# The last phase of a streaming encoder layer: o and z loaded apart, y in halves from a bound, gates read a step ahead

## The chip, the cores and the metric

The kernel runs on one core of a Trainium2 chip. The metric is device time in microseconds (us) of one execution; the number for a kernel is the median of several. Beside it one execution was taken by the hardware profiler: its span is the time from the first to the last instruction of the program, its own time includes what lies around that.

A core has five engines with an instruction queue each, worked off in order: TensorE (PE, with PEld for its weight loads), VectorE (DVE), ScalarE (ACT), GpSimd (POOL) and SyncE (SP). In this kernel nearly all DMAs are issued by SP, so an issue that waits holds up every DMA issue behind it.

## The reference, cut to what matters

One layer, for 2,048 prompt frames and 8 sample streams of 16 frames, `D_MODEL` = 1024. The attention outputs `oa`, `ob` and the projections `za`, `zb`, `ga`, `gb` are there; the last phase computes:

```python
def merge_branches(oa, ob, za, zb, ga, gb, subln_g, lam_init, w_branch_a, w_branch_b, w_out):
    oa = rms_norm(oa, subln_g) * (1.0 - lam_init)
    ya = (oa.reshape(b, s, WIDTH_A) * jax.nn.silu(za)) @ w_branch_a
    yb = (ob.reshape(b, s, WIDTH_B) * jax.nn.silu(zb)) @ w_branch_b
    return (jax.nn.sigmoid(ga) * ya + jax.nn.sigmoid(gb) * yb) @ w_out
...
        xp = xp + gate * merge_branches(...)
...
    y_prompt = rms_norm(xp, final_g)
```

`WIDTH_A` = `WIDTH_B` = 512. The same is done for the sample frames.

## The kernel before, in words

All tensors are float32. A matmul operand is split into two float16 parts, hi and lo, after a scaling by a power of two (`scales` makes it from a sum of squares, with tiny DVE instructions; `split` writes hi on ACT or POOL and lo on DVE, L284 to L292). A product is then three chains of matmuls: hi x hi, hi x lo, lo x hi.

The program has two large parts. The first projects tiles of 128 frames and runs both attentions for eight units; it writes each tile's attention output to `o_d`, z to `z_d` and the gates' pre-activations to `g_d` in HBM. The second, the last phase (from L1305 on, `with ExitStack() as c2`), takes 17 tiles (`tiles`: 15 prompt tiles, the sample tile NT = 16, then the last prompt tile) through a pipeline, one step n for each:

- `inputs(t)` (L1160): loads o, z and g; u = o * z * sigmoid(z), normed for the first half by `orms`. POOL multiplies o by z in two halves (L1175), ACT takes sigmoid of z into a PSUM bank of kind "mm" (L120 is the helper `act`), DVE multiplies (L1177, L1181). ACT takes the sigmoid of the gates in place. Then the sum of squares (L274), the scale, and the split of u into `u16` (L287, L292), which lies in `hs[2]`; o and z lie in `hs[0]` and `hs[1]`.
- `turned(st)` (L1193): a DMA transpose of `u16` into `st["u"]`, one of two buffers.
- `branches(st)` (L1198): four pieces (half j of the columns, branch br) of 12 matmuls (L1207); DVE scales by `iu` and multiplies by the gate (L1209), POOL adds the two branches (L1211). After the last, `finish` squares both halves on ACT, makes the scale `sy`, and splits y into `y16`.
- `turned_y(st)` (L1230): one DMA transpose of `y16` into the one buffer `L["y"]`.
- `output(t, st)` (L1331): loads the x rows (L1337), two halves of 24 matmuls with w_out (L1344), DVE scales by `iy` and the adaLN gate (L1348), POOL adds x (L1352), then ACT squares, DVE makes the root and scales (L1357), and the rows are stored (L1358).

Tiles overlap: step n multiplies the branches of tile n, the output of tile n - 1, and prepares tile n + 2. The pieces of a step have costs, and `interleave` merges them by these with those of a second stream, `lane`: the attention of the sample streams (`sample`, L701), spread over steps 0 to 12 (`S_TILES` = 13). It loads cache tiles of 512 KB, transposes keys on TensorE (L735, copied out at L736), makes scores (L745, L752), weights (L770, L776), and values (L788), with sigmoid, scan (L607) and products of its own on ACT, DVE and POOL. The program order made so is what a scheduler with a simulated timeline starts from; from there each engine has a fixed order.

PSUM has eight banks, by kind: "mm" 2, "s" 3, "t" 1, "o" 2. The sample stream's queries (L721) and weights `wn` (L776) take "t", of which there is one.

`early_work` puts the inputs of the first two tiles and the branches of the first among the last attention steps. Step order of the pieces before:

```python
            if 0 < n <= NT:
                work += branches(states[tiles[n]])
            if n + 1 <= NT:
                work.insert(2, (0.9, lambda n=n: turned(states[tiles[n + 1]])))
            if n + 2 <= NT:
                work.insert(5, (0.1, lambda n=n: states.update({tiles[n + 2]: inputs(tiles[n + 2])})))
            if n > 0:
                work += output(tiles[n - 1], states.pop(tiles[n - 1]))
            if 0 < n <= NT:
                work.append((0.9, lambda n=n: turned_y(states[tiles[n]])))
```

## Time and profile before

| | |
|---|---|
| median of 3 runs | 2289.36 us (2288.38 to 2291.46) |
| profiled execution, its own time | 2288.94 us |
| its span | 2287.2 us, mean granted TensorE clock 0.966 |
| first and last matmul of the branches (L1207) | 1752.6 and 2249.8 us |
| first and last matmul of the output (L1344) | 1792.7 and 2276.3 us |

Busy time is given by engine; PE's includes the depth of its pipeline. A row of waits names the engine and line that stood idle, then what ended the wait. In rows of the trace a square bracket gives the idle time before an instruction and what released it; "issue" means that nothing the profile shows was waited for. Tile names are those of the buffers: `wa`, `wb` are the 4 KB buffers in which the last phase keeps gates, y16, u and y transposed and the branch weights; `hs` holds o, z and u16; `dk`, `dks`, `dsc` belong to the sample stream. The granted clock is TensorE's, as a share of full speed.

### The profile page before, as it was taken

The page shows a single profiled execution, that of the slowest core. Times are in us where ns is not written, and L with a number is a line of the kernel's source. Part 1 is how long each engine was busy: PE and PEld are TensorE (multiplying, and loading weights), DVE is VectorE, ACT ScalarE, POOL GpSimd, SP SyncE. Part 2 cuts the span into 40 slices and gives each one's busy share as a digit, 9 for nine tenths or more (in the row PEclk, how much of TensorE's full clock was granted, in tenths as well). Part 3 has the DMA queues.
Part 4 walks back from the last instruction along what each step waited for, and adds up shares of the span by engine and source line. Part 5 has one row for each costly group of instructions (what it writes and reads, how often), then busy time and mean ns, then how long its engine had stood idle before and what let it go on. Part 6 is the DMA issues. An engine that isn't in the chain of part 4 may idle for free.

```text
span 2287.2 us, 40620 instructions
## 1 busy us (share of the span) xinstructions
PE 2083.3 (91%) x14478; PEld 1111.4 (49%) x14478; DVE 1606.7 (70%) x3523; ACT 1483.5 (65%) x2968; POOL 689.8 (30%) x575
## 2 busy tenths in 40 slices
PE   4998999998999999899989989999986789988997
PEld 2554554554555455455545545555543344444443
DVE  4668666788886678978667797876777655555654
ACT  3877677788767677877667777666776444444431
POOL 1522013255301235530023463012344222232331
PEclk7998999999999999999999999999996899999998
DMA  8667668697775778875576887657687989887662
GB/s 295 212 214 184 151 144 219 155 211 171 190 161 121 168 144 205 178 187 124 124 174 147 193 179 176 150 138 167 145 184 171 295 220 253 213 222 199 186 157 74
DMA packets 764267, 411.93 MB, mean 180 GB/s; under 512 B 525498, under 2 KB 709098, under 8 KB 763552
## 3 DMA queue, kind: packets, MB, share of 16 engines
q1 hardware_dynamic: 762986, 408.86, 72.9%
q8 instruction: 113, 1.85, 0.3%
q14 instruction: 90, 0.74, 0.1%
q10 hardware_dynamic: 1078, 0.48, 0.1%
HBM read 211.53 MB, written 72.91 MB: 124 GB/s over the span
## 4 chain that ended last, share of the span: by engine, by line
PE 57%; DVE 13%; DMA 9%; ACT 8%; issue 8%; POOL 3%; SPq 1%; POOLq 0%; DVEq 0%; ACTq 0%
PE ps_mm L423 20%; PE ps_mm L495 12%; PE ps_mm L1207 5%; PE ps_o L1344 5%; PE ps_s L630 3%; PE ps_s L631 3%; DVE sc_n L607 3%; DMA wt<-sc_n 2%; ACT junk L274 2%; ACT sc_p L120 1%; PE ps_o L682 1%; DMA wb<-wa 1%; POOL sc_p L613 1%; DMA hs<-o_d 1%; DVE wb L292 1%
## 5 line engine op out<-in xcount | busy, mean ns | idle before, releaser
L423 PE MATMUL ps_mm<-wb,hs 128*128 128x512 f16 x2244 | 559.6, 382 | 7.3 <-DVE v L292 3.9
L613 POOL TENSOR_TENSOR sc_p<-sc_p,sc_n 128x127 f32<-128x127 f32 (+7 forms) x192 | 306.9, 1603 | 779.7 <-DVE sc_n L607 769.9
L423 PEld LDWEIGHTS <-hs 128*128 128x128 f16 x2928 | 256.7, 98 | 237.1 <-issue 14.8
L495 PE MATMUL ps_mm<-wa,hs 128*128 128x512 f16 x1224 | 307.4, 379 | 0.0
L607 DVE TENSOR_TENSOR_SCAN sc_n<-ps_s,sc_n,zero_t 128x512 f32<-128x512 f32 x192 | 245.5, 1279 | 68.2 <-ACT ps_s L120 66.1
L120 ACT ACTIVATE sc_p<-ps_s,usc 128x512 f32<-128x512 f32 (+3 forms) x320 | 202.6, 633 | 98.3 <-PE ps_s L631 60.6
L630 PE MATMUL ps_s<-k,qst 128*128 128x512 f16 (+3 forms) x640 | 226.4, 354 | 40.3 <-DVE sc_n L607 36.9
L562 DVE TENSOR_TENSOR sc_n<-sc_p,sc_n 128x128 f16<-128x128 f32 (+7 forms) x192 | 212.0, 1110 | 41.2 <-ACT sc_n L561 40.8
L631 PE MATMUL ps_s<-k,qst 128*128 128x512 f16 (+3 forms) x640 | 226.6, 355 | 0.0
L1344 PE MATMUL ps_o<-wo,wb 128*128 128x512 f16 x816 | 195.8, 395 | 24.5 <-DMA wb<-wa 21.1
L682 PE MATMUL ps_o<-v,wt 128*128 128x128 f16 x1088 | 192.1, 224 | 25.1 <-DMA wt<-sc_n 25.0
L495 PEld LDWEIGHTS <-hs 128*128 128x128 f16 x1632 | 140.2, 98 | 119.7 <-issue 0.5
L120 ACT ACTIVATE ps_s<-ps_s,usc 128x512 f32<-128x512 f32 (+3 forms) x320 | 194.2, 607 | 0.0
L561 ACT CAST sc_n<-sc_p 128x128 f16<-128x128 f32 (+7 forms) x192 | 153.6, 805 | 57.6 <-POOL sc_p L613 57.4
L683 PE MATMUL ps_o<-v,wt 128*128 128x64 f16 x1088 | 173.3, 197 | 0.0
L423 PE MATMUL ps_mm<-wa,hs 128*128 128x512 f16 x684 | 168.9, 379 | 0.0
L682 PEld LDWEIGHTS <-wt 128*128 128x128 f16 x1088 | 106.7, 101 | 106.7 <-DMA wt<-sc_n 33.9
L1344 PEld LDWEIGHTS <-wb 128*128 128x128 f16 x816 | 81.1, 101 | 127.8 <-DMA wb<-wa 24.3
L683 PEld LDWEIGHTS <-wt 128*128 128x128 f16 x1088 | 104.7, 100 | 72.2 <-issue 1.4
L457 POOL TENSOR_TENSOR rot<-pr,rope 128x256 f32<-128x256 f32 x68 | 63.3, 931 | 251.4 <-ACT pr L437 204.3
L607 DVE TENSOR_TENSOR_SCAN sc_n<-ps_s,zero_t 128x128 f32<-128x128 f32 (+3 forms) x128 | 104.6, 818 | 47.4 <-ACT ps_s L120 46.1
L274 ACT ACTIVATE junk<-wa 128x1024 f16<-128x1024 f32 (+1 forms) x73 | 66.7, 914 | 103.9 <-POOL wa L1211 66.5
(328 smaller groups left out, 4273.7 us busy)
## 6 DMA issues: line engine op xcount, KB each, us to landing
hs<-hT_d SPq DMA_DIRECT2D x122, 512.0 KB, 4.2
g_d<-gt SPq DMA_DIRECT2D x68, 256.0 KB, 3.8
wa<-in_w_in_dram SPq DMA_DIRECT2D x52, 256.0 KB, 5.0
out_dram<-pr SPq DMA_DIRECT2D x204, 64.0 KB, 1.8
wa<-g_d SPq DMA_DIRECT2D x25, 512.0 KB, 5.4
wide<-in_w_ada_dram SPq DMA_DIRECT2D x12, 1024.0 KB, 8.4
z_d<-pr SPq DMA_DIRECT2D x136, 64.0 KB, 2.0
o_d<-o SPq DMA_DIRECT2D x136, 64.0 KB, 2.6
```

The lines of the kernel that those rows point to most:

```text
L120: i = S.activation(**kw)
L423: T.matmul(box["p"], box["h"][:, hi, k, :], U["w"][k][:, wi, :], start=(n == 0), stop=(n == 3 * KT - 1))
L495: T.matmul(box["g"][:, 0:gw], box["h"][:, hi, k, :], U["wg"][k // per][:, k % per, wi, :], start=(j == 0), stop=(j == 3 * KT - 1))
L561: S.copy(out=hi, in_=src)
L562: V.tensor_tensor(out=lo, in0=src, in1=hi, op=ALU.subtract)
L607: V.tensor_tensor_scan(out=dst[:, lo : lo + n][:, ::-1], data0=src[:, 0:n][:, ::-1], data1=zero_t[:, 0:1].to_broadcast([P, n]), initial=fi ...
L613: G.tensor_tensor(out=p[:, 0:m], in0=p[:, 0:m], in1=n[:, 1 : m + 1], op=ALU.mult)
L630: T.matmul(p[:, 0:n], qst[:, c, :], kk[:, c, 0:n], start=True, stop=False)
L631: T.matmul(p[:, 0:n], qst[:, 2 + c, :], kk[:, c, 0:n], start=False, stop=not diag)
L682: T.matmul(po[:, c * P : (c + 1) * P], wt[:, wj, :], vt[:, c, :, :], start=first, stop=False)
L683: T.matmul(po[:, c * P : c * P + 64], wt[:, nb + wj, :], vt[:, c, 0, :], start=False, stop=last)
L1344: T.matmul(po, st["y"][:, yi * 8 + k, :], wo[j * 4 + k // 2][:, wi, k % 2, :], start=(n == 0), stop=(n == 3 * KT - 1))
```

## The change

- o is loaded at the start of a step (`started`), z after the second branch piece; `inputs` then works on both. POOL multiplies o by z in one instruction, placed in its order after POOL's last sum of the branches (`L["sum"]`, an order without a wait); DVE's multiplications come after the last split of y (`L["low"]`).
- sigmoid of z is written over z, no more into a PSUM bank, and `u16` then takes z's buffer `hs[1]`.
- y's scale comes from a bound, the sum of squares of u times that of the branch weights (`wf`), so `sy` and `iy` are made in `inputs`; each half of y is split as soon as it is summed, into the gate buffer that it has freed, and has a transpose of its own. The transposed y has two buffers. The output's matmuls go through the k of half 0 first.
- the rows of a tile are normed (`normed`) and stored (`stored`) a step later; x is loaded a step before it is used, into three buffers in turn (`hs[2]` is the third).
- gates are loaded at the end of step n for tile n + 2 (`gated`), and their sigmoid is taken in step n + 1 (`opened`).
- the transposition of u moves from the middle of the step after to the end of the same step.
- in the sample stream, the transposes of queries and of `wn` take a bank "s" instead of "t".

```diff
@@ queries, weights
-            pt = bank("t")
+            pt = bank("s")
@@
+    def started(t):
+        m = len(begun) % 2
+        begun.append(t)
+        load(out=hs[0], in_=o_d[t])
+        return dict(t=t, u=L["u"][m], home=L["g"][2 * m : 2 * m + 2], yT=L["y"][m])
+
-    def inputs(t):
+    def inputs(st):
         o, z = hs[0:2]
-        load(out=o, in_=o_d[t])
-        load(out=z, in_=z_d[t])
...
-        for n in range(2):
-            c = slice(n * 512, (n + 1) * 512)
-            sg = bank("mm")
-            act(out=sg, in_=z[:, c], func=AF.Sigmoid)
-            G.tensor_tensor(out=o[:, c], in0=o[:, c], in1=z[:, c], op=ALU.mult)
-            if n == 1:
-                V.tensor_tensor(out=o[:, c], in0=o[:, c], in1=sg, op=ALU.mult)
...
-        for g in gs:
-            act(out=g, in_=g, func=AF.Sigmoid)
+        i = G.tensor_tensor(out=o, in0=o, in1=z, op=ALU.mult)
+        if "sum" in L:
+            tc.add_manual_dep(i.ins, L["sum"].ins.name, NOSYNC, reason="order of tiles")
+        act(out=z, in_=z, func=AF.Sigmoid)
+        for h in range(4):
+            c = slice(h * P, (h + 1) * P)
+            i = V.scalar_tensor_tensor(out=o[:, c], in0=z[:, c], scalar=r[:, h : h + 1], in1=o[:, c], op0=ALU.mult, op1=ALU.mult)
+            if "low" in L:
+                tc.add_manual_dep(i.ins, L["low"].ins.name, NOSYNC, reason="order of tiles")
+        V.tensor_tensor(out=o[:, 512:D], in0=o[:, 512:D], in1=z[:, 512:D], op=ALU.mult)
...
+        V.tensor_tensor(out=yb, in0=acc, in1=L["wf"], op=ALU.mult)
+        sy = scales(yb, tiny, "sy")
...
-        u16 = hs[2].bitcast(F16).rearrange("p (f n) -> p f n", f=2)
+        u16 = z.bitcast(F16).rearrange("p (f n) -> p f n", f=2)
...
+    def gated(st):
+        st["g"] = [b.rearrange("p (b n) -> p b n", b=2) for b in st["home"]]
+        for j in range(2):
+            load(out=st["g"][j], in_=g_d[st["t"]].rearrange("p (b n) -> p b n", b=2)[:, :, j * 512 : (j + 1) * 512])
+
+    def opened(st):
+        for g in st["g"]:
+            act(out=g, in_=g, func=AF.Sigmoid)
@@ branches
-                G.tensor_tensor(out=g, in0=st["g"][j][:, 0, :], in1=g, op=ALU.add)
-                if j == 1:
-                    finish()
-        def finish():
...
+                L["sum"] = G.tensor_tensor(out=g, in0=st["g"][j][:, 0, :], in1=g, op=ALU.add)
+                y16 = st["home"][j].bitcast(F16)[:, 0:D]
+                L["low"] = split(y16[:, 0:512], y16[:, 512:D], g, st["sy"][:, 0:1], S)
@@
-    def turned_y(st):
-        st["y"] = yT = L["y"].bitcast(F16).rearrange("p (k n) -> p k n", n=P)
-        nc.sync.dma_start_transpose(out=yT, in_=st["y16"].rearrange("p f n -> p (f n)"))
+    def turned_y(st, j):
+        st["y"] = yT = st["yT"].bitcast(F16).rearrange("p (k n) -> p k n", n=P)
+        nc.sync.dma_start_transpose(out=yT[:, j * KT : (j + 1) * KT, :], in_=st["home"][j].bitcast(F16)[:, 0:D])
@@ early_work
-            states[t] = inputs(t)
-            if t == tiles[0]:
-                turned(states[t])
+            states[t] = started(t)
+            load(out=hs[1], in_=z_d[t])
+            inputs(states[t])
+            turned(states[t])
+            gated(states[t])
+            opened(states[t])
@@ output
-                for yi, wi in ((0, 0), (0, 1), (1, 0)):
-                    for k in range(KT):
-                        T.matmul(po, st["y"][:, yi * 8 + k, :], wo[j * 4 + k // 2][:, wi, k % 2, :], start=(n == 0), stop=(n == 3 * KT - 1))
+                for half, yi, wi in [(half, yi, wi) for half in range(2) for yi, wi in ((0, 0), (0, 1), (1, 0))]:
+                    for k in range(half * 4, half * 4 + 4):
+                        T.matmul(po, st["y"][:, half * KT + yi * 4 + k % 4, :], wo[j * 4 + k // 2][:, wi, k % 2, :], start=(n == 0), stop=(n == 3 * KT - 1))
...
-                    load(out=y_rows(t), in_=x)
+                    late.append((x, t))
@@ the steps
+            work = [(0.1, lambda: states.update({new: started(new)}))] if more else []
+            work += fro[:2] + [(0.1, normed)]
+            if more:
+                work.append((0.1, lambda: load(out=hs[1], in_=z_d[new])))
+            work += fro[2:] + to[:1] + [(0.1, stored)]
+            if 0 < n < NT:
+                work.append((0.1, lambda: opened(states[tiles[n + 1]])))
+            if n <= NT:
+                work.append((0.1, lambda: with_x(n)))
+            if more:
+                work.append((0.1, lambda: inputs(states[new])))
+            if fro:
+                work.append((0.5, lambda: turned_y(states[tiles[n]], 0)))
+            work += to[1:]
+            if fro:
+                work.append((0.5, lambda: turned_y(states[tiles[n]], 1)))
+            if more:
+                work.append((0.9, lambda: turned(states[new])))
+                work.append((0.1, lambda: gated(states[new])))
             interleave(work, aside(n))
+        normed()
+        stored()
```

`fro` are the four branch pieces of tile n, `to` the two output halves of tile n - 1, and `new` is tile n + 2.

More of the change, by code (lines that the diff above doesn't have):

```diff
@@ L774, in weights @@
                     in_=pt.rearrange("p (j i r s) -> p j i r s", j=4, r=2, s=NS)[:, :, :, r, :])
-            pt = bank("t")
+            pt = bank("s")
             T.transpose(pt[:, 0:P], w[:, 512:640], ident)
@@ L1241, in branch_weight @@
         if i == 0:
-            L["s"] = [scales(total(add_up(wsums[:, lo : lo + 8], 8)), con, f"s_w{lo}") for lo in (0, 8)]
+            sums = [total(add_up(wsums[:, lo : lo + 8], 8)) for lo in (0, 8)]
+            L["wf"] = con.tile([P, 1], F32, name="wf")
+            V.tensor_copy(out=L["wf"], in_=sums[0])
+            L["s"] = [scales(x, con, f"s_w{lo}") for x, lo in zip(sums, (0, 8))]
             L["sa"] = con.tile([P, 1], F32, name="sa")
@@ L1329, in gate_rows, with with_x, normed, stored @@
             return pg
+        def with_x(n):
+            t = tiles[n]
+            states[t]["x"] = x = hs[2] if n % 3 == 2 else s2.tile([P, D], F32, tag="x", name="x2", bufs=2)
+            load(out=x, in_=x_rows(t))
+        late, ready = [], []
+        def normed():
+            while late:
+                x, t = late.pop(0)
+                acc = tiny.tile([P, 1], F32, tag="facc", name="facc")
+                sum_squares(x, D, acc)
+                r = rsqrt_one(acc, D, tiny, "rF")
+                V.scalar_tensor_tensor(out=x, in0=x, scalar=r, in1=fg, op0=ALU.mult, op1=ALU.mult)
+                ready.append((x, t))
+        def stored():
+            while ready:
+                x, t = ready.pop(0)
+                load(out=y_rows(t), in_=x)
         def output(t, st):
-            box = {}
             def half(j):
-                if j == 0:
-                    box["x"] = s2.tile([P, D], F32, tag="x", name="x2", bufs=2)
-                    load(out=box["x"], in_=x_rows(t))
-                x = box["x"]
+                x = st["x"]
                 c = slice(j * 512, (j + 1) * 512)
```

53 lines of the change are left out of this document (13 added, 40 removed).

## The prediction

> **What bounds the kernel now.** I read the page first, then the busy time by stage, then the two lines of matmuls of the last phase, then who waited for whom in it, and last the instructions in order of time around the longest waits.
>
> ```profile
> span 2287.2 us, 40620 instructions
> PE 2083.3 (91%) x14478; PEld 1111.4 (49%) x14478; DVE 1606.7 (70%) x3523; ACT 1483.5 (65%) x2968; POOL 689.8 (30%) x575
> ```
>
> The diff touches only what runs after 1752.6 us (first matmul of L1207) and a little just before it, so I split that part: first two tiles, the tiles that share their steps with the sample stream, the tiles without it, and the end.
>
> ```profile
> core 0: us, PE busy (x) PEld busy (x) DVE busy (x) ACT busy (x) POOL busy (x), PEclk, DMA share, GB/s
> 1752.60:1800.00 47.40, 37.78 (x189) 17.41 (x190) 26.79 (x56) 18.88 (x30) 14.88 (x14) 0.86 0.99 263
> 1800.00:2166.40 366.40, 322.83 (x2469) 170.12 (x2468) 209.31 (x569) 162.99 (x311) 107.13 (x78) 0.95 0.85 222
> 2166.40:2250.10 83.70, 80.52 (x376) 36.22 (x373) 47.33 (x124) 28.53 (x48) 23.21 (x18) 1.00 0.56 147
> 2250.10:2287.20 37.10, 23.31 (x90) 9.17 (x87) 12.96 (x36) 5.62 (x10) 6.28 (x5) 0.83 0.18 56
> ```
>
> TensorE is the fullest engine in every stage, but between 1800 and 2166.4 it idles 366.4 - 322.8 = 43.6 us and its granted clock is 0.95. DVE, ACT and POOL are far from full; the DMA share of 0.85 is high. The same stage for L1207 alone and then for L1344 alone (busy time and count are PE's), and one row of L1344:
>
> ```profile
> 1800.00:2166.40 366.40, 125.08 (x528) 52.03 (x528) 0.95 0.85 222
> 1800.00:2166.40 366.40, 127.21 (x529) 52.14 (x528) 0.95 0.85 222
> L1344 PE MATMUL ps_o<-wo,wb x816: 379/379/634, 1792.7 to 2276.3; 128*128 128x512 f16 x164
> 2229.27 8.15 PE L1344 MATMUL ps_o<-wo,wb 128*128 128x512 f16 x37
> ```
>
> A tile has 48 matmuls of each line, so 528/48 = 11 tiles take 366.4 us, 33.3 us each. At full speed 37 matmuls take 8.15 us, so one start to the next is (8.15 - 0.379)/36 = 0.216 us. The stage's 1,057 matmuls need 228 us, the other PE work 322.8 - 125.1 - 127.2 = 70.5 us: a floor of 299 us, 27.2 us a tile. The stage after it, without the sample stream, has almost no slack (80.5 of 83.7 busy). So the gain to be had lies in the 67 us between 366 and 299, plus the two ends. What PE waits for from 1752 us on:
>
> ```profile
> PE ps_o L1344 <- DMA wb<-wa: 21.1, 8, 4.8
> PE ps_s L735 <- DVE dsc L607: 10.7, 3, 5.5
> PE ps_t L776 <- DVE dks L736: 10.2, 2, 5.1
> ```
>
> and what the queues behind these waits stand for (engine and line, what was waited for: us, times, longest):
>
> ```profile
> ACT wa L120 <- DMA wa<-g_d: 46.8, 20, 6.4
> ACT wb L120 <- DMA wb<-g_d: 26.0, 7, 9.3
> POOL hs L1175 <- DMA hs<-o_d: 57.5, 8, 13.2
> SPq L1358 <- DVE x L1357: 73.6, 12, 18.4
> SPq L1337 <- DMA out_dram<-x: 38.4, 13, 5.8
> ```
>
> **The change, part by part.**
>
> *Price of an idle gap.* After a gap of 5.1 us:
>
> ```profile
> 2007.03 0.48 PE L776 MATMUL ps_t<-ident,dsc 128*128 128x128 f32 x1 [5.12 <-DVE dks L736]
> 2007.29 7.27 PE L1344 MATMUL ps_o<-wo,wb 128*128 128x512 f16 x23
> 2004.80:2011.60 6.80, 4.58 (x12) 1.76 (x13) 4.71 (x17) 3.85 (x9) 2.04 (x2) 0.50 0.51 154
> ```
>
> The granted clock is 0.50 for 6.8 us, and 23 matmuls take 7.27 us where 22 x 0.216 + 0.379 = 5.13 would do: 2.1 us more. At the end of the kernel it is 7.66 - 5.13 = 2.5. I take 2.3 us for each gap of 3 us or more.
>
> *y in halves from a bound.* Before, both halves of g must be squared and summed before either is split, and one transpose carries the whole tile. At the end it reads:
>
> ```profile
> 1900.98 1.46 PE L1344 MATMUL ps_o<-wo,wb 128*128 128x512 f16 x3 [4.03 <-DMA wb<-wa]
> 2250.19 0.75 DVE L1209 SCALAR_TENSOR_TENSOR wa<-ps_mm,iu,wa 128x512 f32<-128x512 f32 x1 [1.84 <-PE ps_mm L1207]
> 2258.17 1.82 SPq L1232 DMA_TRANSPOSE wb<-wa  x1
> 2262.47 7.66 PE L1344 MATMUL ps_o<-wo,wb 128*128 128x512 f16 x23 [3.29 <-DMA wb<-wa]
> ```
>
> From the last scaling (2250.2) to the landing (2262.5) are 12.3 us, covered by only 37 matmuls of the tile before. The change drops the squares on ACT and their sum, splits half 0 while half 1 is still multiplied, and gives yT a second buffer. The chain shrinks to scaling 0.75, POOL's sum 1.25 (half of the 2.49 for two such below), ACT's split 0.7 and DVE's 0.75 (estimates, from the 1,024-wide ones below), landing 4.3 (2258.2 to 2262.5): 7.8 us for the last half, which 8 us of matmuls cover. It could remove all 21.1 us of the eight waits, and three of them are long enough to halve the clock (4.8, 4.03, 3.29): 3 x 2.3 = 6.9, together 28.0. The least is the end and the row at 1901 alone, 3.3 + 4.0 + 4.6 = 12. I take 24: the first wait also stands behind the loads of w_out. The cost is 17 more transposes on SP's queue: 1.82 us at the least for a whole one bounds a half's issue to 0 to 1.8, at most 31 us of SP time, beside a queue that now stands 73.6 + 38.4 us for rows to be normalised and stored. "A step later" and the third x buffer take those two away. I cost the issues at nothing; without that cover each would delay the load behind it by up to 1.8 us.
>
> *Gates one step ahead.* Now ACT stands in order for a gate:
>
> ```profile
> 1852.80 1.06 ACT L120 ACTIVATE wb<-wb 128x1024 f32<-128x1024 f32 x1 [9.35 <-DMA wb<-g_d]
> 1855.76 0.42 DVE L607 TENSOR_TENSOR_SCAN dsc<-ps_s,zero_t 128x128 f32<-128x128 f32 x1 [10.59 <-ACT ps_s L120]
> 1858.10 1.97 PE L735 MATMUL ps_s<-ident,dk 128*128 128x128 f32 x8 [5.51 <-DVE dsc L607]
> 2049.19 1.11 PE L735 MATMUL ps_s<-ident,dk 128*128 128x128 f32 x4 [3.06 <-DVE dsc L607]
> ```
>
> The sample stream's sigmoids stand behind it on ACT, the scan behind those on DVE, and the scan holds the three "s" banks that TensorE needs. That is the 10.7 us of three gaps, two of them over 3 us: 10.7 + 4.6 = 15.3. With the load issued a step earlier ACT does not wait. Bounds 0 (ACT waits for POOL's sum instead) and 15.3; I take 13.
>
> *o and z apart, sigmoid of z in place, order of tiles, two transposes moved from bank "t" to "s".* The gap at 2007 has this chain:
>
> ```profile
> 1996.62 2.49 POOL L1175 TENSOR_TENSOR hs<-hs,hs 128x512 f32<-128x512 f32 x2 [12.31 <-issue]
> 2003.10 1.13 DVE L1181 SCALAR_TENSOR_TENSOR hs<-ps_mm,orms,hs 128x128 f32<-128x128 f32 x4 [8.30 <-ACT ps_mm L120]
> 2006.29 0.68 DVE L736 COPY dks<-ps_t 128x512 f32<-128x512 f32 x1
> ```
>
> POOL stands with the product of the next tile, its sum for the present tile behind it; ACT and DVE follow, and the copy that frees bank "t" comes last. Now the product is put behind the sum, and DVE's four scalings behind the split. The two such gaps cost 10.2 + 4.6 = 14.8. But the moved transposes now share three banks with scan and scores, so the gain is between -5 (one more such gap) and 14.8; I take 7.
>
> *Work itself.* One product of 1,024 instead of two of 512 on POOL, one sigmoid instead of two, four more tiny DVE instructions: nothing on the path, hidden under 27 us of matmuls a tile.
>
> *What is late next.* z's buffer now becomes u16, so the next z can be loaded only when u's transpose has landed. These rows (landing of z; ACT square and split; DVE scalings and split; landing of u's transpose) price the ring:
>
> ```profile
> hs<-z_d SPq DMA_DIRECT2D x12, 512.0 KB, 7.0
> L274 ACT ACTIVATE junk<-hs 128x1024 f16<-128x1024 f32 x16 | 16.9, 1057 | 5.9 <-DVE hs L1177 5.3
> L287 ACT ACTIVATE hs<-hs,su 128x1024 f16<-128x1024 f32 x16 | 18.2, 1137 | 1.3 <-DVE su L225 1.3
> L1181 DVE SCALAR_TENSOR_TENSOR hs<-ps_mm,orms,hs x56: 337/343/352, 1767.2 to 2208.5; 128x128 f32<-128x128 f32 x56
> L292 DVE SCALAR_TENSOR_TENSOR hs<-hs,su,hs x16: 1277/1284/2306, 1757.6 to 2217.5; 128x1024 f16<-128x1024 f32 x16
> DMA to landing us min/median/max: 4.4/6.5/7.5
> ```
>
> 7.0 + 2.5 (product) + 4 x 0.34 + 0.69 (an estimate: half a 1,024 operation of 1.28, rounded up) + 1.06 + about 1 (five tiny instructions) + 1.14 + 1.28 + 6.5 = 22.5 us. My step would be (366.4 - about 35)/11 = 30 us, so the ring has 7 us to spare and I cost it at 0, with up to 3 us a tile (33 us) if each of its seven hops stands in a queue for 1.5 us.
>
> L1181 reads PSUM now and is steady (337 to 352 ns); L292 reads two SBUF tensors and reaches 2,306 against 1,277. The scalings become such operations, so they may take 1.8 times as long, at most 1.6 us a tile more, inside the ring's slack. The Trainium skill's page "SBUF — State Buffer", section "Who interferes with whom", gives the reason: a DVE operation with two SBUF inputs contends with a POOL operation that reads SBUF, and the one issued second is blocked for the whole of the other. The spread of L292 agrees; by that rule alone the sum would lose at most 11 x 1.6 = 18 us, and only if the ring binds.
>
> *Before 1752 us.* Two tiles are now fully opened and turned in the last attention steps, with a transpose and gate loads on SP among the attention's own. No row shows it; the nearest are PE's 9.6 us of idle in the first stage (47.4 - 37.8). Bounds -6 (a better start) and +12 (two landings of 6.5 us, with SP standing); I take +3.
>
> *Sum:* 24 + 13 + 7 - 3 = 41 us. The profiled execution took 2288.94 us, 0.4 below the median of the runs, so about 2248.
>
> **The rivals.**
>
> *Half a gain.* TensorE's y waits go, but ACT, DVE and POOL only change the instruction they stand for, since all three stay in order and the sample stream's banks do not grow. For it: of ACT's 72.8 us on gates TensorE felt only 10.7. Then about 19 of y (between 12 and 28) less the 3 before 1752 us: -16, 2273.
>
> *TensorE at its floor.* All gaps close: 28.0 + 15.3 + 14.8 and 7 us of small ones, -65, 2224. Against it: with some 60 of that in the sampled stage its DMA share would become 0.85 x 366/306 = 1.02.
>
> *The ring binds, slower.* Each lap of z, u16 and its transpose takes longer than today's 33.3 us a tile; SP, in order, then holds loads, y's transposes and sample caches behind the waiting transpose. It decides once the seven hops queue for more than 33.3 - 22.5 = 10.8 us. At 37 us a tile: 11 x 3.7 = 41, less 9 still saved behind 2166 us (3.3 + 2.5 at the end, 3.2 in the stage ahead of it): 2321. For it: POOL's 57.5 us on o show how a late load is felt. Against: u is turned two steps ahead.
>
> *Nothing.* The waits are covered otherwise: the removed PE gaps come back as others, 2289.
>
> **How the numbers follow.** A measurement of this kernel tells some 0.2%, 4.6 us. Forecast 0.52 (own range 2230 to 2264), half a gain 0.20, floor 0.12, ring 0.09, nothing 0.07. Faster is 0.84 less 0.02 of the half gain's edge, 0.82; the same 0.08; slower 0.10. The range 2222 to 2281 holds all but the ring, nothing and a little of both tails.
>
> **What would show it.** Right: no wait of L1344 for its transpose over 2 us, no ACT wait for a gate over 2 us, 1800 to 2166 shortened by about a tenth at a granted clock near 1.0, DMA share above 0.9. Wrong: SP standing for u's split with PE idle behind it, long idle of L735 or L776 for "s" banks, PE waiting at L1207 for u, or the first matmul of the branches later than 1760 us.

## The result, and the profile after

The changed kernel took 2307.38 us (median of 6 runs, 2298.81 to 2314.08), the kernel before 2292.36 beside it (6 runs, 2288.38 to 2298.03): ratio 1.0069, 95% interval 1.0049 to 1.0089. It is slower by 0.7%; 2248 us were forecast, and 2307 lies above the range. The profiled execution took 2307.38 us itself, span 2305.5.

The profile after, page and stages (the sampled stage, the tiles without the sample stream, the end); then where three lines end (the last scores of attention L630, its last product L683, the last matmul of the sample stream L788), after and before:

```profile
span 2305.5 us, 40451 instructions
PE 2095.0 (91%) x14478; PEld 1114.4 (48%) x14478; DVE 1607.6 (70%) x3524; ACT 1458.1 (63%) x2883; POOL 679.3 (29%) x558
...
1800.00:2180.40 380.40, 340.28 (x2524) 177.43 (x2526) 220.42 (x575) 151.87 (x261) 102.18 (x69) 0.94 0.90 229
2180.40:2268.00 87.60, 76.14 (x343) 33.08 (x333) 43.43 (x122) 23.61 (x33) 21.86 (x15) 0.92 0.55 131
2268.00:2305.50 37.50, 25.82 (x113) 10.91 (x111) 13.11 (x31) 4.85 (x8) 6.28 (x5) 0.88 0.19 57
...
L630 PE MATMUL ps_s<-k,qst x640: 219/379/634, 98.4 to 1763.4; 128*128 128x512 f16 x92, 128*128 128x128 f16 x28, 128*128 128x384 f16 x28, 128*128 128x256 f16 x12
L683 PE MATMUL ps_o<-v,wt x1088: 191/193/261, 326.1 to 1784.7; 128*128 128x64 f16 x182
L788 PE MATMUL ps_s<-dv,wz x768: 219/219/297, 1854.6 to 2180.4; 128*32 128x64 f32 x128, 128*32 128x128 f32 x64
```

```profile
L630 PE MATMUL ps_s<-k,qst x640: 216/379/634, 97.0 to 1742.3; 128*128 128x512 f16 x92, 128*128 128x128 f16 x28, 128*128 128x384 f16 x28, 128*128 128x256 f16 x12
L683 PE MATMUL ps_o<-v,wt x1088: 191/193/261, 324.7 to 1766.5; 128*128 128x64 f16 x182
L788 PE MATMUL ps_s<-dv,wz x768: 219/219/297, 1832.9 to 2166.2; 128*32 128x64 f32 x128, 128*32 128x128 f32 x64
```

Read the last start in each row. The same marks for the two experiments that matter most below:

| us from the span's start | before | after | gates behind the split | and the first tiles as before |
|---|---|---|---|---|
| last score (L630) | 1742.3 | 1763.4 | 1763.1 | 1742.9 |
| last attention product (L683) | 1766.5 | 1784.7 | 1785.4 | 1766.9 |
| last sample matmul (L788) | 2166.2 | 2180.4 | 2153.0 | 2145.6 |
| end of the span | 2287.2 | 2305.5 | 2260.6 | 2253.2 |

After minus before: 18.2 us are lost before attention ends; the sampled stage takes 395.7 instead of 399.7 (4.0 gained); what follows takes 125.1 instead of 121.0 (4.1 lost). Sum 18.3, the difference of the spans. So there are two questions: who delays attention's end, and why the last phase, which should have become 44 us shorter (41 and the 3 that were charged before 1752), did not.

**The last phase.** What PE, ACT and SP waited for after the change, from 1815 us on (engine and line, what ended the wait: us, times, longest):

```profile
PE ps_s L776 <- ACT dks L736: 12.9, 2, 7.6
PE ps_s L735 <- ACT dks L736: 5.8, 1, 5.8
PE ps_mm L1221 <- DVE r L261: 5.8, 2, 2.9
PE ps_mm L1221 <- DVE r L265: 4.7, 1, 4.7
...
ACT wa L120 <- DMA wa<-g_d: 31.2, 8, 5.6
ACT wb L120 <- DMA wb<-g_d: 28.5, 4, 8.7
...
SPq L1200 <- DMA wa<-wa: 26.4, 10, 4.2
SPq L1200 <- DMA wb<-wa: 23.9, 7, 4.4
SPq L1200 <- DMA wb<-wb: 11.3, 6, 3.2
```

The output's matmuls (now L1369) hardly wait for y any more: that row stood first before, with 21.1 us, and is down to 1.2. But ACT still stands for gates, 59.7 us in all, and now PE feels it. One such place in order of time:

```profile
2053.12 1.60 SPq L1200 DMA_DIRECT2D wb<-g_d  x1
2054.77 2.13 SPq L1233 DMA_TRANSPOSE wb<-wa  x1
2060.43 1.06 ACT L120 ACTIVATE wb<-wb 128x1024 f32<-128x1024 f32 x1 [8.22 <-DMA wb<-g_d]
2061.33 0.53 SPq L1200 DMA_DIRECT2D wa<-g_d  x1
2065.48 1.06 ACT L120 ACTIVATE wa<-wa 128x1024 f32<-128x1024 f32 x1 [4.00 <-DMA wa<-g_d]
2066.45 0.57 ACT L736 COPY dks<-ps_s 128x512 f32<-128x512 f32 x1
2067.07 0.47 PE L776 MATMUL ps_s<-ident,dsc 128*128 128x128 f32 x1 [7.61 <-ACT dks L736]
```

Read it upwards. PE idles 7.61 us because L776 needs an "s" bank that ACT's copy L736 frees; the copy takes 0.57 us but stands on ACT behind two sigmoids of gates; each of these waits for a load that SP has only just issued. The second load is issued 8 us after the first, since the gates of the tile two on go into the buffer out of which y of the present tile is being transposed, and SP waits for that transpose (the three rows of L1200). The change loads the gates earlier in the code, but at the twelve waits of the two ACT rows the scheduler had put the sigmoid into ACT's order next to its load; the slack in the source became none on the engine. In the tail the same thing reaches PE by another way:

```profile
2187.28 1.06 ACT L120 ACTIVATE wa<-wa 128x1024 f32<-128x1024 f32 x1 [2.88 <-DMA wa<-g_d]
2188.24 1.13 ACT L287 ACTIVATE hs<-hs,su 128x1024 f16<-128x1024 f32 x1
2189.40 1.28 DVE L292 SCALAR_TENSOR_TENSOR hs<-hs,su,hs 128x1024 f16<-128x1024 f32 x1 [3.67 <-ACT hs L287]
2192.98 1.01 PE L1221 MATMUL ps_mm<-wa,wb 128*128 128x512 f16 x2 [4.68 <-DVE r L265]
```

ACT's split of u stands behind the gate, DVE's half of that split behind ACT, and behind that on DVE the scaling (L1223) whose "mm" bank PE needs. The profile puts the wait down to L265, a tiny instruction of the row norm that stood between them.

**The end of attention.** After, then before (POOL, ACT and SP; L613 is attention's, L1172 and before L1175 are the product of o and z of the second tile):

```profile
1737.71 2.03 SPq L1210 DMA_TRANSPOSE wa<-hs  x1
1742.36 0.32 SPq L1264 DMA_DIRECT2D hs<-z_d  x1
1747.09 2.35 POOL L1172 TENSOR_TENSOR hs<-hs,hs 128x1024 f32<-128x1024 f32 x1 [15.45 <-DMA hs<-z_d]
1749.47 1.06 ACT L120 ACTIVATE hs<-hs 128x1024 f32<-128x1024 f32 x1 [7.96 <-POOL hs L1172]
1752.33 0.67 ACT L120 ACTIVATE sc_p<-ps_s,usc 128x512 f32<-128x512 f32 x1
1755.01 2.00 POOL L613 TENSOR_TENSOR sc_p<-sc_p,sc_n 128x1023 f32<-128x1023 f32 x1 [0.69 <-DVE sc_n L607]
```

```profile
1722.92 1.12 SPq L1164 DMA_DIRECT2D hs<-z_d  x1
1730.14 1.18 ACT L120 ACTIVATE ps_mm<-hs 128x512 f32<-128x512 f32 x2
1744.72 1.99 POOL L613 TENSOR_TENSOR sc_p<-sc_p,sc_n 128x1023 f32<-128x1023 f32 x1 [4.67 <-DVE sc_n L607]
1747.89 2.49 POOL L1175 TENSOR_TENSOR hs<-hs,hs 128x512 f32<-128x512 f32 x2 [1.18 <-DMA hs<-o_d]
```

Before, the second tile's z was loaded at 1722.9, into a buffer that was free as soon as the first tile's product and sigmoid had read it. Its own sigmoid was in PSUM at 1731, and POOL took its product at 1747.9, behind attention's additions. Now z waits for the transpose of the first tile's u (1737.7), is loaded at 1742.4, and POOL stands 15.45 us with the product, attention's next additions behind it. The sigmoid in place must wait for that product, since it overwrites z, and attention's sigmoids stand behind it, and behind two of gates, on ACT until 1752. The Trainium skill says that the queues of ScalarE, VectorE and GpSimdE are strictly first in, first out ("PSUM — Partial Sum Buffer", "Engine vs sequencer instructions"). Both episodes agree: the 0.57 us copy above and attention's additions here stood behind an instruction that was not ready.

### The profile page after: what moved, and what is told of

The parts are those of the page before. It is cut to its first block, busy times and chain, and to the rows that moved or that the text cites. A ratio compares the mean times of both kernels' runs of the same rounds, so it can differ in the third digit from the quotient of the medians.

```text
span 2305.5 us, 40451 instructions
## 1 busy us (share of the span) xinstructions
PE 2095.0 (91%) x14478; PEld 1114.4 (48%) x14478; DVE 1607.6 (70%) x3524; ACT 1458.1 (63%) x2883; POOL 679.3 (29%) x558
## 5 line engine op out<-in xcount | busy, mean ns | idle before, releaser
L613 POOL TENSOR_TENSOR sc_p<-sc_p,sc_n 128x127 f32<-128x127 f32 (+7 forms) x192 | 305.9, 1597 | 782.1 <-DVE sc_n L607 772.2
L630 PE MATMUL ps_s<-k,qst 128*128 128x512 f16 (+3 forms) x640 | 225.5, 353 | 40.2 <-DVE sc_n L607 33.2
L682 PE MATMUL ps_o<-v,wt 128*128 128x128 f16 x1088 | 191.8, 224 | 33.3 <-DMA wt<-sc_n 33.3
L683 PE MATMUL ps_o<-v,wt 128*128 128x64 f16 x1088 | 173.0, 197 | 0.0
L683 PEld LDWEIGHTS <-wt 128*128 128x128 f16 x1088 | 104.6, 100 | 73.0 <-issue 2.8
L545 DVE TENSOR_SCALAR_CACHE_REDUCE sc_n<-ps_s,usc 128x512 f32<-128x512 f32 (+3 forms) x148 | 98.9, 669 | 41.6 <-PE ps_s L631 27.0
L437 ACT ACTIVATE pr<-ps_mm,usc 128x512 f32<-128x512 f32 (+1 forms) x136 | 86.4, 635 | 59.4 <-PE ps_mm L423 59.0
L678 PE MATMUL ps_o<-v,wt 128*128 128x128 f16 x544 | 105.2, 223 | 19.4 <-DMA wt<-sc_n 13.0
```

The source lines that it names most:

```text
L613: G.tensor_tensor(out=p[:, 0:m], in0=p[:, 0:m], in1=n[:, 1 : m + 1], op=ALU.mult)
L630: T.matmul(p[:, 0:n], qst[:, c, :], kk[:, c, 0:n], start=True, stop=False)
L678: T.matmul(po[:, 0:P], wt[:, wj, :], vt[:, :, 0, :], start=first, stop=False)
L682: T.matmul(po[:, c * P : (c + 1) * P], wt[:, wj, :], vt[:, c, :, :], start=first, stop=False)
L683: T.matmul(po[:, c * P : c * P + 64], wt[:, nb + wj, :], vt[:, c, 0, :], start=False, stop=last)
```

## The experiments

All ratios are to the kernel before on the same chip, with 95% intervals. My first theory for the early loss was the ring (u16 in z's buffer); for the last phase, that the gates' order on ACT counts. The rivals were SP's early transpose and the norms, which delay DVE.

**e1: the first tile's u16 in a buffer of its own.**

```
-        u16 = z.bitcast(F16).rearrange("p (f n) -> p f n", f=2)
+        u16 = (hs[2] if t == tiles[0] else z).bitcast(F16).rearrange("p (f n) -> p f n", f=2)
```

> Edit: only for the first tile u16 is written to the third x buffer instead of z's buffer, so the z of the second tile need not wait for the first transpose of u. Ring theory (in the changed kernel POOL's product of the second tile waits 15.4 us for that z, ACT's sigmoid 8.0 us for the product, and the last attention scores stand behind both): the last score matmul (1763.4 us in the changed kernel, 1742.3 before) comes back to 1742 to 1750, and the time falls by 13 to 20 us against the changed kernel, to a ratio of about 0.998 to 1.001 against the kernel before. Rival (the additional transposes and gate loads on SP's queue hold up the attention's own transposes): the last score stays at 1758 or later and the gain is under 6 us.

2303.38 us, 1.0061 (1.0038 to 1.0083): no gain that can be measured, and the last score is at 1765.3. z was now loaded early, at 1728.9, and POOL waited for o instead. The first tile's split had read o's buffer by 1737.6, but the load of o then stood on SP behind transposes until 1741.6. The sigmoid starts as POOL ends, though its row names a DMA:

```profile
1746.64 2.34 POOL L1172 TENSOR_TENSOR hs<-hs,hs 128x1024 f32<-128x1024 f32 x1 [13.29 <-DMA hs<-o_d]
1749.02 1.06 ACT L120 ACTIVATE hs<-hs 128x1024 f32<-128x1024 f32 x1 [5.87 <-DMA o_d<-o]
```

So the ring alone is not it, and the rival's reading, the queue of SP, is not excluded by this run.

**e2: the second tile's u transposed only at the start of the last phase.**

```
-            turned(states[t])
+            if t == tiles[0]:
+                turned(states[t])
...
+            work = [(0.9, lambda: turned(states[tiles[1]]))] if n == 0 else []
```

> Edit: the transpose of the second tile's u is taken out of the attention's last steps and put at the start of the last phase, as it was before the change; z and u16 still share a buffer. Ring theory: z of the second tile waits as before, so the last score matmul stays at 1760 us or later and the time stays within 5 us of the changed kernel (ratio 1.004 to 1.009 against the kernel before). Rival (the additional issues on SP are the cost): the last score comes back to 1742 to 1750 and 13 us or more are gained.

2307.14 us, 1.0072 (1.0049 to 1.0095), last score 1769.2. SP's extra transpose costs nothing that can be measured.

**e3: gates behind the split.** An order without a wait puts the gates' sigmoids of the next tile behind the last split of y of the present one on ACT, and `opened` moves to the step's end.

```
         for g in st["g"]:
-            act(out=g, in_=g, func=AF.Sigmoid)
+            i = act(out=g, in_=g, func=AF.Sigmoid)
+            if len(begun) > 2:
+                tc.add_manual_dep(i.ins, L["hi"].ins.name, NOSYNC, reason="gates after the split")
```

> Edit: on ACT the two sigmoids of the next tile's gates are put, by an order without a wait, behind the last split of y of the present tile; the loads stay where they are. Theory (the early load was never used: the sigmoids stand in ACT's order right behind their own load, which waits for y's transpose in the same buffer, so ACT stands 59.7 us for gates and holds the copies that free the banks of kind s, and the splits before the second scaling): ACT's waits for gates fall below 10 us, TensorE's waits for the copy L736 (18.7 us) and for DVE at L1221 (10.5 us) mostly go, 25 to 40 us are gained, a ratio of 0.990 to 0.996 against the kernel before. Rival (ACT only stands for POOL's sum of the branches instead, 68 us in the changed kernel already): under 8 us gained.

2266.05 us, 0.9903 (0.9881 to 0.9925): against the changed kernel's 1.0069 a gain of 1.66%, 38 us. No wait of ACT for a gate is left. By the table above the sampled stage falls to 367.6 us and the rest to 107.6; attention ends as late as before the edit. This separates the two losses.

**e4: the row norms of the tile before moved behind the first output half.**

```
-            work += fro[:2] + [(0.1, normed)]
+            work += fro[:2]
...
-            work += fro[2:] + to[:1] + [(0.1, stored)]
+            work += fro[2:] + to[:1] + [(0.1, normed), (0.1, stored)]
```

> Edit: the norm of a finished tile's rows is put behind the four branch pieces and the first output half instead of after two branch pieces. Theory of the late gates: DVE's chain of the norm was only the last to end; what is late ahead of it is the split of u behind ACT's wait for gates, so the time stays within 5 us of the changed kernel. Rival (the norm on DVE stands ahead of the scaling that frees the banks of kind mm and makes the unsampled tiles 25 to 28 us long instead of 20 to 23): those tiles come back to 23 us or less and 10 to 20 us are gained, a ratio of 0.998 to 1.003.

2307.6 us, 1.0082 (1.0062 to 1.0103). The norm named in the tail's wait was only what stood between; ACT's 57 us for gates stayed.

**e5: the first two tiles as before.** On top of e3 and e1: their sigmoid goes into PSUM by halves, their product by halves.

```
+        if len(begun) < 3:
+            for n in range(2):
...
+                act(out=sg, in_=z[:, c], func=AF.Sigmoid)
+                G.tensor_tensor(out=o[:, c], in0=o[:, c], in1=z[:, c], op=ALU.mult)
```

> On top of the gates' order of e3_gates_after_split and the first tile's u16 of its own (e1): for the first two tiles alone the sigmoid of z goes into two PSUM halves, with the product o*z by halves, as in the kernel before; the later tiles stay in place. Theory A (in place is what costs the early 20 us: ACT's sigmoid of tile 1 waits for POOL's product, which waits for a load that is held by tile 0): the last score matmul returns from 1763 to 1742-1750 us, the end falls by 13-20 us against e3's 2266 to 2246-2253, ratio to before 0.981-0.985. Theory B (the early pieces' number and place: three pieces in the last attention step, so tile 1's first work is interleaved sooner): the last score stays at 1760 or later, 2262-2270, ratio 0.988-0.992.

2256.98 us, 0.9851 (0.9834 to 0.9869). The last score is back at 1742.9, as theory A said; the end fell by 0.52%, 12 us, a little less than the 13 to 20 expected. POOL's product of the second tile now comes behind attention's addition of 1744.4:

```profile
1748.30 2.59 POOL L1177 TENSOR_TENSOR hs<-hs,hs 128x512 f32<-128x512 f32 x2 [0.84 <-DMA hs<-o_d]
```

**e6: nine early pieces as before** (on e3; both early transposes of y in one piece).

```
-... + [lambda j=j: turned_y(states[tiles[0]], j) for j in range(2)]
+... + [lambda: [turned_y(states[tiles[0]], j) for j in range(2)]]
```

> On top of e3_gates_after_split: the two early transposes of y's halves form one piece, so that there are nine early pieces as before and the last attention step takes tile 1's inputs and one branch half, not two. Theory A (in place and shared buffers): last score stays at 1760 or later, 2262-2270, ratio 0.988-0.992. Theory B (number and place of the pieces): last score 1742-1752, 2246-2256, ratio 0.981-0.986.

2273.57 us, 0.9927 (0.9902 to 0.9951), last score 1767.2. Theory B falls: POOL's product stands 15.9 us, as long as in the changed kernel, a little later.

**e7: the second tile's inputs as the last early piece** (on e3; only its o and z are still loaded at the old place; the four calls form `begin`).

```
-            inputs(states[t])
-            turned(states[t])
-            gated(states[t])
-            opened(states[t])
+            if t == tiles[0]:
+                begin(t)
...
             L["first"][i]()
+            if i == 5:
+                begin(tiles[1])
```

> On top of e3_gates_after_split: tile 1's o and z are loaded at their old place, but its product, sigmoid, scaling, split, transpose and gate loads form the last of the early pieces, behind the first tile's branches, in the step after the last attention step. Theory A and the general form of it (work of tile 1 stands on POOL and ACT ahead of attention's last products and sigmoids while it waits for a load): whatever tile 1 waits for, nothing of attention stands behind it; last score 1742-1752, and 2246-2256 (0.981-0.986), unless the first step of the last phase then waits for u of tile 1 (up to +6). Rival C (the early loss is not tile 1's standing but more work before 1760, such as eight 128-column scalings in SBUF and two y transposes): last score stays at 1758 or later, 2262-2270.

2259.41 us, 0.9867 (0.9848 to 0.9886), last score 1743.7; the score came back as expected, the time is 3 us above the range. Here z is in place and u16 in z's buffer as in the change; only the order differs, and POOL's product waits for nothing:

```profile
1762.12 2.34 POOL L1172 TENSOR_TENSOR hs<-hs,hs 128x1024 f32<-128x1024 f32 x1
```

**e8: the "t" bank again** (on e3), and **e9: the "s" bank alone in the kernel before**, the same two lines of `queries` and of the last score block the other way round.

```
-            pt = bank("s")
+            pt = bank("t")
```

> On top of e3_gates_after_split: the sampled stage's transposes of queries and of the last score block use the t bank again, as before, not s. If the move of banks was worth the 7 us that the prediction gave it (between -5 and +14.8): 2266+7 = 2273, ratio 0.993, with L735 or L776's matmuls waiting for t banks. If it is worth nothing: 2263-2269, ratio 0.989-0.991. If s was the worse bank (its own buffers wait for ACT's copies): 2256-2262.

> The kernel before with one part of the change alone: the transposes of queries and of the last score block use the s bank. Theory: the bank is worth its own 14 us (e8 against e3 gave 0.62%) whatever else is there: 2273-2281, ratio 0.993-0.997. Rival: the bank counts only once y's and the gates' waits are gone: 2286-2292, 0.998-1.002.

e8 2282.8 us, 0.9965 (0.9953 to 0.9977); e9 2290.86, 1.001 (0.9998 to 1.0021). In e9 the wait of L776 for its bank (10.2 us before) is down to 1.1, but L735 waits 23.3 us for "s" banks instead of 10.7: the wait moved.

```profile
PE ps_s L735 <- DVE dsc L607: 15.5, 3, 6.0
PE ps_s L735 <- ACT dks L736: 7.8, 3, 2.9
PE ps_s L776 <- ACT dks L736: 1.1, 2, 0.7
```

e8 lost 14 us against e3, outside all three expectations. The waits that the prediction named did not bring it: no wait of L776 came back, and L721 waits 2.3 us for "t". New are one wait of L735 for ACT (6.6 us) and one for y's transpose (5.1), and from 1815 on POOL's product waits for z 47.3 us, 26.8 in e3. Which of these carries the 14 us stays open. The same two lines are worth nothing measurable in the kernel before (e9), so the bank has no price that holds in both kernels.

**e10: only the gates' order, in the kernel before** (the order itself as in e3).

```
-        for g in gs:
-            act(out=g, in_=g, func=AF.Sigmoid)
+        if len(begun) < 3:
+            opened(gs)
...
+                work.append((0.1, lambda n=n: opened(states[tiles[n + 1]]["g"])))
```

> The kernel before with the gates' order alone: the gates' sigmoids of the next tile are put behind the last split of y of the present tile on ACT, everything else as before (y in one transpose, t bank, sigmoid of z in PSUM). Theory: ACT standing for gate loads costs what the prediction read from the waits, 13 to 20 us: 2269-2276, ratio 0.991-0.994. Rival: y's wait takes its place, since y still stands on PE's path: 2284-2292, 0.997-1.001.

2279.92 us, 0.9958 (0.9941 to 0.9974): about 10 us, between the two expectations. Most of the waits for y stay; before, then here, both from 1815 on:

```profile
PE ps_o L1344 <- DMA wb<-wa: 16.3, 7, 4.0
PE ps_o L1352 <- DMA wb<-wa: 12.7, 7, 4.0
```

**e11: e5 without e1's buffer.** This run tells place and buffer apart.

```
-        u16 = (hs[2] if t == tiles[0] else z).bitcast(F16).rearrange("p (f n) -> p f n", f=2)
+        u16 = z.bitcast(F16).rearrange("p (f n) -> p f n", f=2)
```

> e5_first_tiles_as_before without the first tile's u16 apart: only the sigmoid of z of the first two tiles goes to PSUM by halves; z and u16 still share their buffer, so tile 1's z is loaded only after the transpose of tile 0's u (1737). If being in place (ACT behind POOL's product) is the cause by itself: last score 1742-1750 and 2255-2262, ratio 0.984-0.988. If the shared buffer is enough to hold POOL or ACT: last score 1755-1765 and 2262-2270, ratio 0.988-0.992.

2263.5 us, 0.9884 (0.987 to 0.9899), last score 1763.3. Now ACT waits for z itself, POOL as before:

```profile
1745.64 2.50 POOL L1177 TENSOR_TENSOR hs<-hs,hs 128x512 f32<-128x512 f32 x2 [14.43 <-DMA hs<-z_d]
1745.57 1.12 ACT L120 ACTIVATE ps_mm<-hs 128x512 f32<-128x512 f32 x2 [4.76 <-DMA hs<-z_d]
```

Neither edit alone brings attention back (e1, e11), both do (e5), and so does the order alone (e7). The cause is a product and a sigmoid that the scheduler places ahead of attention's last ones while their data hang on the first tile: through z's buffer, through o's, or through the sigmoid's wait for the product. Before and in e5 the second tile's o is loaded no earlier (1743.2 and 1743.9, after the change 1739.8); there the product only stands behind attention's additions. Why the scheduler places it there with both edits and not with one, no run shows.

**e12: e7 with u16 apart.**

```
-        u16 = z.bitcast(F16).rearrange("p (f n) -> p f n", f=2)
+        u16 = (hs[2] if t == tiles[0] else z).bitcast(F16).rearrange("p (f n) -> p f n", f=2)
```

> e7_second_inputs_last and the first tile's u16 in its own buffer: tile 1's z is loaded early too. If u of tile 1 is what the first step of the last phase waits for in e7 (first branch tiles 45 and 28 us apart): 2252-2257, ratio 0.983-0.9855. If the first 50 us of the last phase are bound by the transfers of the output weights (DMA share 1.0 there): 2256-2262, as e7, 0.985-0.988.

2257.36 us, 0.9856 (0.9835 to 0.9877): not to be told from e7.

Then the two halves of the prediction's largest term, y, and the third x buffer were taken out of e5 one at a time. **e13: both transposes of y at the end of the step. e14: two x buffers. e17: y's scale from its own sum.**

```
e13          work += to[1:]
             if fro:
+                work += [(0.5, lambda j=j: turned_y(states[tiles[n]], j)) for j in range(2)]
e14 -... x = hs[2] if n % 3 == 2 else s2.tile([P, D], F32, tag="x", name="x2", bufs=2)
    +... x = s2.tile([P, D], F32, tag="x", name="x2", bufs=2)
e17 +                if j == 1:
    +                    for i in range(2):
    +                        sum_squares(st["g"][i][:, 1, :], 512, acc[:, i : i + 1])
    +                    sy = scales(add_up(acc, 2), tiny, "sy")
...
    +                    for i in range(2):
    +                        y16 = st["home"][i].bitcast(F16)[:, 0:D]
    +                        L["low"] = split(y16[:, 0:512], y16[:, 512:D], st["g"][i][:, 1, :], sy[:, 0:1], S)
```

> On top of e5_first_tiles_as_before (2257): both transposes of y stand at the end of the step, so the first half is no longer turned ahead of the second output half; bounds, buffers and everything else stay. If turning the first half early carries part of y's 28 us, the output's matmuls wait for the transpose again (about 6 us at one tile in three): +10 to +20, 2267-2277, ratio 0.989-0.994. If the bound alone (the split no longer behind a whole-row sum) carries it: within 5 of e5, 2252-2262, 0.983-0.987.

> On top of e5_first_tiles_as_before (2257): two x buffers instead of three, with rows still finished a step later. If the third buffer is needed: a tile's x is loaded only after the store of the tile two before, POOL's addition to x waits for the load and the output's bank with it: +10 to +30, 2267-2287, 0.989-0.998. If the loads come in time with two: 2253-2261, 0.984-0.987.

> On top of e5_first_tiles_as_before (2257, 0.985): y's scale comes again from y's own sum of squares (two squares on ACT, then the scale, then both splits behind the second branch half of block b), not from the bound known with u. All else stays, the gates' order too. If the bound is what the prediction's 24 us for y came from: the output's matmuls wait for y's transposes again, 15 to 24 us more, 2272-2281, ratio 0.991-0.996. If the gates' order and the tile order carry it: 2253-2264, 0.983-0.988.

e13 2252.89 us, 0.9831 (0.9811 to 0.9852); e14 2256.1, 0.9843 (0.9827 to 0.9859); e17 2254.37, 0.9844 (0.982 to 0.9867). None is slower than e5. In e17 the waits on PE longest in sum are for the sample stream's caches, and no wait for y's transpose is among them:

```profile
PE ps_t L735 <- DMA dk<-in_cache_b_k_dram: 8.7, 4, 3.9
PE ps_t L735 <- DMA dk<-in_cache_a_k_dram: 6.5, 2, 4.9
PE ps_o L682 <- DMA wt<-sc_n: 5.3, 1, 5.3
```

In e13, too, no wait for y's transpose is on PE. So neither the bound, nor the early half, nor the third x buffer carries a measurable gain alone. That one of them covers for another isn't excluded, since each was taken out by itself.

**e15: e5 and e7 together. e16: e12 with the two gate rows moved up, ahead of the loop that cuts the output's weights. e18: e15 and e13 together.**

```
e15              L["first"][i]()
+                if i == 5:
+                    begin(tiles[1])
e16 +        for n in range(2):
    +            S.copy(out=gate[:, n * 512 : (n + 1) * 512], in_=gate_rows(0, n))
```

> e5_first_tiles_as_before and e7_second_inputs_last together. If both cure the same standing of POOL and ACT: no further gain, 2252-2260, 0.984-0.987, with the last score at 1742-1745. If something of tile 1 is still in attention's way in e5: last attention matmul at 1760 instead of 1767, and 2248-2253, 0.982-0.984.

> e12_second_last_u16_apart with the two gate rows (their loads, the selecting matmuls and copies) ahead of the output's weights: PE waited 11.4 and 11.6 us for these two small loads behind the weights' transfers at the start of the last phase. If that wait is on the path: 2246-2253, 0.981-0.984. If the first 50 us are bound by the weights' transfers and not by what PE waits for: 2254-2261, 0.9845-0.988.

> The fastest parts together: the first two tiles' sigmoids in PSUM and u16 apart (e5), tile 1's inputs as the last early piece (e7), y's two transposes at the end of the step (e13). If e13's 2253 is a gain of its own: 2246-2254, 0.980-0.983. If e5, e13, e14 and e15 differ only by how their instructions happen to lie: 2250-2259, 0.982-0.986.

e15 2255.9 us, 0.9836 (0.9816 to 0.9856): attention ends at 1760.5 instead of 1766.9 and no measurable time is gained. e16 2263.22, 0.9874 (0.9854 to 0.9893), above both expectations: no gain over e12, whose interval it overlaps, and its last score stays at 1742.8. e18 2255.32, 0.9852 (0.9831 to 0.9873): the parts do not add up. e5, e12, e13, e14, e15, e17 and e18 all lie between 0.983 and 0.986, with overlapping intervals. They beat the kernel before by 1.4 to 1.7%, and the changed kernel by more than 2%; I would not rank them.

What holds them there is not shown; no run moves fewer bytes. What speaks for the transfers is the 200 us from 1850 to 2050, before and in e3, and e5's longest waits on PE after 1815:

```profile
1850.00:2050.00 200.00, 173.90 (x1299) 91.99 (x1298) 111.51 (x298) 89.91 (x172) 54.72 (x41) 0.95 0.88 227
...
1850.00:2050.00 200.00, 186.81 (x1475) 100.34 (x1472) 137.87 (x356) 90.90 (x162) 57.34 (x39) 0.98 0.99 254
...
PE ps_t L735 <- DMA dk<-in_cache_a_k_dram: 7.2, 2, 4.4
PE ps_s L735 <- DMA dk<-in_cache_b_k_dram: 5.9, 3, 2.4
```

The DMA share goes from 0.88 to 0.99 (0.98 in e5), and the sample stream now waits for its caches, as it did nowhere in the prediction's rows. It would also explain why 20 us earlier in attention give only 12 at the end: between the last attention product and the last sample matmul e5 takes 378.7 us where e3 takes 367.6.

## Why the prediction was wrong

- **Gates one step ahead** failed, and it decides the sign. The step read: "With the load issued a step earlier ACT does not wait", worth 13 us, bounds 0 and 15.3. ACT waited 59.7 us after 1815, and putting the sigmoids behind the split gained 38 us (e3). The prediction moved the load in the code and took the sigmoid's place in ACT's order for granted; it also did not count that the load's new buffer is the one y is transposed from. Its lower bound of 0 had a reason for no gain (ACT waits for POOL's sum instead), and none that excludes a loss. Read from before, the 15.3 us of gaps were not far off: the gates' order alone gave 10 there (e10).
- **Before 1752 us** failed in size: +3 taken, bounds -6 and +12, measured +18.2. It listed SP's transposes and PE's idle time, the latter from the stage behind 1752, and left out POOL and ACT, where the second tile's product and sigmoid stood ahead of attention's. Curing it gained 8 to 12 us at the end, not 18 (e7, e5 against e3).
- **y**: the waits went as predicted, 21.1 to 1.2 us, both from 1752 on. But the step's working isn't shown to carry it: without the bound (e17) and without the early half (e13) they stay away, though either may cover for the other. The gates held at most a small part of y (e10, 16.3 to 12.7 us). What is left is the second buffer of the transposed y and the order of tiles; neither was run alone.
- **Bank and order of tiles**, 7 us from -5 to 14.8: the bank alone is worth nothing measurable in the kernel before (e9), since L735 then waits where L776 did. On top of e3, taking it back costs 14 us (e8), but not by the waits that the step priced. That the sample stream's banks do not grow stood among the rivals, under half a gain. The order of tiles wasn't run.
- **The ring** cost little in the last phase: in e3 PE waits for u's transposes 5.3 us in all; no run takes it out of the later tiles. Its sum of 22.5 us left out the sigmoid of z, which in place stands between the product and the scalings: another 1.06 us, 23.6. It took part once, in attention's last step, where no slack of 33 us a tile stands beside it. The rival that "the ring binds, slower" had the right sign, but not the mechanism.
- **SBUF operands**: the scalings' median went from 343 to 346 ns (L1181, now L1178), the longest from 352 to 1378. In four of the 17 tiles the four scalings took 2.15 us instead of 1.14, in two more 1.36 and 1.49, and in all six a POOL instruction ran beside them (at 1845.0 the sum L1225, from 1844.4 to 1846.2). That agrees with the section of the Trainium skill that the prediction cited ("SBUF — State Buffer", "Who interferes with whom"). It is some 4.6 us of DVE time in all, not the 18 given at most.
- **Price of a gap**: after the 7.61 us above the granted clock was 0.50 from 2067 to 2071 and 0.94 in the microsecond after, so some 2.1 us were lost. The 2.3 taken were about right.
- **The rival "half a gain"** named the mechanism that won, engines in order that only change what they stand for, but priced it as less gain, not as a loss.
- **The signs**: "ACT wait for a gate" showed the failure; "first branch matmul later than 1760" did not. It came at 1742.4, where before it came at 1752.6, because the first tile's matmuls were interleaved into the attention that had been delayed. A mark on the delayed work itself, the last score, would have told.

With both orders mended (e5, e7, e12, e15) the design reaches 0.984 to 0.987, 2252 to 2259 us on the median of 2289.36 shown before. That this is near the 2248 forecast is in part luck: the gates' place on ACT alone makes 38 us where 13 were counted, and of the 24 for y neither half shows a gain alone.

## What to carry to other kernels

A load issued earlier helps only if its consumer's place on an in-order engine moves with it or stays behind everything that is ready sooner: look at what stands behind the consumer on its engine, and pin the order if a scheduler chooses it. When work is pulled into the last steps of another stage, list for every engine what it will stand in front of, and follow each operand's buffer to whoever still holds it. Once one wait is cured, take the parts out of the cured version one by one: y's bound, its early half and the third x buffer were each, alone, worth nothing measurable here.

## What the runs showed of the hardware that I had not expected

The same edit, the gates' sigmoids behind the split, was worth 10 us in the kernel before (e10) and 38 us in the changed one (e3), though ACT stood longer for gates in the former (72.8 us) than in the latter (59.7, both from 1752 on). In these two kernels the sum of an engine's waits says little about their price; what stands behind them does. The dip of the clock cost less than the gap ahead of it: 7.61 us idle, then four at 0.50, some 2 us of work.
